# Latent attention's queries: rotary columns of four heads in one tile

## The chip, the core and the metric

The kernel runs on one core of a Trainium2 chip. The metric is the time of one execution on the device in microseconds, as the median of several runs. The core's engines are TensorE (PE in the profile; its weight loads are PEld), VectorE (DVE), ScalarE (ACT), GpSimd (POOL) and SyncE (SP). SP, ACT and POOL also issue transfers (DMA), each in its own queue and in order.

## What is computed

The reference is a two-layer encoder over 512 tokens with 1024 features. In each layer a feed-forward block is followed by three attention branches that are gated and merged, by a second feed-forward block and by a gated input embedding. The change lies in the first branch, latent attention with 16 heads:

```
q = (rms_norm(c_q, q_norm) @ w_uq).reshape(b, s, 16, 64 + 32)
q_nope, q_rope = q[..., :64], apply_rope(q[..., 64:], cos, sin)
k_rope = apply_rope(k_rope, cos, sin)                     # one for all heads
logits = (q_nope . k_nope + q_rope . k_rope) * 96 ** -0.5
```

`c_q` has 384 columns. `apply_rope` takes the 32 rotary columns as two halves x1, x2 of 16 and gives `[x1 cos - x2 sin, x2 cos + x1 sin]`.

## The kernel before

Tokens lie along the free dimension: a tile is 128 features by 512 tokens. Every matrix is split into a rounded part (`h`) and a remainder (`l`), and a product is three matmuls (`mm3`): high times high, low times high, high times low. A queries' tile of 128 features from the three tiles of `cq` takes nine matmuls of 128x512.

`mix` runs the attention branches of a layer. It walks over 16 heads of latent attention, then 8 and 16 heads of the other two. For each head it writes logits (`m0A4s` is layer 0, head 4, the logits of one block of queries), reduces, exponentials, transposes (`m0A4t`) and the product with the values (`m0A4o`). Between them it pumps projections out of a queue, the `Filler`: each has a due head, a name, its count of matmuls ("units") and a generator. `pace` derives from units and due heads how many matmuls go beside each head. The projections of latent attention are `mla_pair(j)` (queries `m0qa` and keys `m0kap` of heads 2j and 2j+1), `mla_v(g)` (values of four heads: four tiles `m0va` of six matmuls of 128x256) and `gate` (`m0ga`, 24 matmuls). Pair 0 and the first values are made before head 0; the other pairs become ready four steps ahead of their heads.

All projections write to PSUM banks of kind "a", of which there are three, taken in turn; logits, transposes and outputs share the five of kind "s". A tile waits until the last reader of its bank is done. ScalarE and VectorE never read a bank at the same time: where both read one, they take turns.

In `mla_pair` before, a head's tile holds its 64 own columns and, in the other half, its rotary columns twice: `[x1 x2 x2 x1]` for even heads, in front of the own columns for odd heads. One multiply by a table (`trig`) of cosines and sines, with the logits' scale in it, evacuates the tile; the key has its rotated columns twice in that half (`KA`, three sets), so the matmul adds the two products. Then the tile is split by ScalarE and VectorE. The keys' tile `m0kap` has two heads: per head ScalarE rounds a half (`m0ka00h`) and VectorE subtracts it (`m0ka00l`).

The weights of each projection come as a chunk of 128x1024 on SP's queue (`wraw`, line 88, four buffers), are rounded by ScalarE (`whi`, line 101) and subtracted by VectorE (`wlo`, line 107) or, during `mix`, negated by ScalarE (line 104) and completed by an adding transfer on POOL's queue (line 105).

The order of instructions on each engine is laid when the program is built, from the order in which the code issues them and from when the planner expects their inputs. On the chip every engine keeps that order.

Of the kernel before, what the change touches and what calls it, by code (L numbers as in the profile page):

```python
# [12 lines left out]
F32 = mybir.dt.float32  # L13
F32R = mybir.dt.float32r
AF = mybir.ActivationFunctionType
ALU = mybir.AluOpType
# [4 lines left out]
P = 128  # L21
D = 1024
KT = D // P
T = 512
# [4 lines left out]
NH = 16  # L29
NHD = 8  # L30
QL = 384
KVL = 256
SCALE_A = 96 ** -0.5
# [149 lines left out]
def encoder_kernel(ctx: ExitStack, tc: tile.TileContext, ins, out):  # L183
    nc = tc.nc
# [22 lines left out]
    def S(name, dt=F32):  # L207
        return sb.tile([P, 512], dt, tag="slot", name=name, bufs=SLOTS)
# [4 lines left out]
    turn = [0]  # L213

    def PS(name, kind=None):


        if kind is None:
            kind = CYCLE[turn[0] % len(CYCLE)]
            turn[0] += 1  # L220
        return psp.tile([P, 512], F32, tag="ps" + kind, name=name, bufs=BANKS[kind])
# [4 lines left out]
    def mm3(ps, lh, ll, rh, rl, start, stop):  # L226
        mm(ps, lh, rh, start, False)
        mm(ps, ll, rh, False, False)
        mm(ps, lh, rl, False, stop)

    def split(src, name, tile=None):

        tile = tile or S
        hi, lo = tile(name + "h", F32R), tile(name + "l", F32R)
        nc.scalar.copy(hi, src)
        nc.vector.tensor_sub(lo, src, hi.bitcast(F32))
        return hi, lo
# [12 lines left out]
    t = S("one")  # L250
# [11 lines left out]
    for l in range(L):  # L262
        for i, at in enumerate((S_F1, S_F2)):
            s = slice(l * 8 + 4 * i, l * 8 + 4 * i + 4)
# [147 lines left out]
    def proj(ps, w, z, i0=0, n=KT, cols=P):  # L412

        wh, wl = w
        for k in range(n):
            c = slice(i0 + k * cols, i0 + k * cols + cols)
            mm3(ps, wh[:, c], wl[:, c], z[k][0], z[k][1], k == 0, k == n - 1)
            if side:
                side.popleft()()
            yield 3  # L420
# [301 lines left out]
    def mix(l, prep, p2):  # L722
        name = f"m{l}"
# [3 lines left out]
        def kept(nm, dt=F32):  # L727
            return stage.tile([P, 512], dt, tag="kept", name=f"{name}{nm}", bufs=17)
# [16 lines left out]
        for d in range(KT):  # L745
            if d % 4 == 0:
                w = W.get(("ple_proj", l, d // 4))
            ps = PS(f"{name}pp{d // 4}{d % 4}")
# [12 lines left out]
        trig = [kept(f"trig{i}") for i in range(3)]  # L761
# [45 lines left out]
        cq, ckv, got = end_q(), [], {}  # L807
# [13 lines left out]
                ckv.extend(end_kv())  # L821

        merged = [None] * KT

        def mla_v(g):
            wh, wl = W.get(("mla_v", l, g))
            vs = [S(f"{name}va{g}_{tb}", F32R) for tb in range(TB)]
            for tb in range(TB):
                ps = PS(f"{name}va{g}_{tb}", "a")[:, 0:256]
                ts = slice(tb * P, (tb + 1) * P)  # L830
                for k in range(2):
                    w = slice(k * 256, (k + 1) * 256)
                    mm(ps, ckv[k][0][:, ts], wh[:, w], k == 0, False)
                    mm(ps, ckv[k][1][:, ts], wh[:, w], False, False)
                    mm(ps, ckv[k][0][:, ts], wl[:, w], False, k == 1)

                v = vs[tb].rearrange("p (g x c) -> p g x c", x=4, c=64)
                src = ps.rearrange("p (g e c) -> p g e c", e=2, c=64)
                nc.scalar.copy(v[:, :, 0::3, :], src)
                nc.vector.tensor_sub(v[:, :, 1:3, :], src, v[:, :, 0::3, :].bitcast(F32))  # L840
                yield 3
            got["va", g] = vs

        def mla_pair(j):
            wh, wl = W.get(("mla_pair", l, j))
            for e in range(2):
                ps = PS(f"{name}qa{j}{e}", "a")
                yield from proj(ps, (wh, wl), cq, i0=e * 384, n=3)
                t = S(f"{name}qa{j}{e}")
                nc.vector.tensor_mul(t, ps, trig[e])  # L850
                got["qa", 2 * j + e] = split(t, f"{name}qa{j}{e}")
            ps = PS(f"{name}kap{j}", "a")
            yield from proj(ps, (wh, wl), ckv, i0=768, n=2)
            for e in range(2):
                r = slice(0, 64) if e == 0 else slice(64, 128)
                kh, kl = KA[j % KSETS][e]
                nc.scalar.copy(kh[r], ps[r])
                nc.vector.tensor_sub(kl[r], ps[r], kh[r].bitcast(F32))

        halves = (slice(0, 64), slice(64, 128))  # L860

        def q_pair(key, at, j):

# [305 lines left out]


        A0, C0, B0, END = 0, NH, NH + NHD, 2 * NH + NHD
        work = [(A0 + 2 * j - 1, ("pair", j), 24, mla_pair(j)) for j in range(8)]
        work += [(A0 + 4 * g, ("va", g), 12, mla_v(g)) for g in range(4)]
        work += [(A0 + 2 * j + 1, ("ga", j), 24, gate("ga", C_GA, j)) for j in range(2, 8)]
        for j in range(8):
# [150 lines left out]
    for l in range(L):  # L1326
# [9 lines left out]
        ffn(l, "ffn1", prep, pm, hooks)  # L1336
        close_stage()
        sums, outs = mix(l, pm, p2)
        open_stage(True)
        pf = Combos(f"f2_{l}", l, S_F2)  # L1340
# [43 lines left out]
KSETS = 3  # L1384
# [13 lines left out]
def _chunk(ins, key):  # L1398

    kind, c = key[0], None  # L1400
    if kind == "cols":
        _, w, l, i = key
        c = ins[w][l][:, i * P:(i + 1) * P].reshape(KT, P, P)
    elif kind == "in":
        _, l, at = key
        c = ins["w_in"][l][:, at:at + P].reshape(KT, P, P)
    elif kind == "down":
        _, w, l, g, i = key
        rows = ins[w + "_w_down"][l][GROUPS[g].start * P:GROUPS[g].stop * P]
        n = rows.shape[0] // P  # L1410
        c = rows[:, i * (1024 // n):(i + 1) * (1024 // n)].reshape(n, P, 1024 // n)
    elif kind == "out":
        _, l, half, kk = key
        c = ins["w_out"][l][kk * 256:(kk + 1) * 256, half * 512:(half + 1) * 512].reshape(2, P, 512)
    elif kind == "rope":
        w = ins["w_in"][key[1]]
        c = np.concatenate([w[:, C_KR:C_KR + 32], w[:, C_KR + 16:C_KR + 32], w[:, C_KR:C_KR + 16]], axis=1).reshape(KT, P, 64)
    elif kind in ("vb", "vc"):
        l, kk = key[1], key[-1]
        at = C_VB if kind == "vb" else C_VC + key[2] * 256  # L1420
        c = ins["w_in"][l][kk * 512:(kk + 1) * 512, at:at + 256].reshape(4, P, 256)
    elif kind == "mla_v":
        _, l, g = key
        w = ins["mla_w_ukv"][l].reshape(KVL, NH, P)[:, 4 * g:4 * g + 4, 64:]
        c = w.reshape(2, P, 256)
    elif kind == "mla_pair":
        _, l, j = key
        parts = []
        for e in range(2):
            w = ins["mla_w_uq"][l][:, (2 * j + e) * 96:(2 * j + e + 1) * 96]  # L1430
            own, rope = w[:, :64], [w[:, 64:], w[:, 80:], w[:, 64:80]]
            w = np.concatenate([own] + rope if e == 0 else rope + [own], axis=1)
            parts.append(w.reshape(3, P, P))
        w = ins["mla_w_ukv"][l].reshape(KVL, NH, P)[:, 2 * j:2 * j + 2, :64].reshape(KVL, P)
        parts.append(w.reshape(2, P, P))
        c = np.concatenate(parts, axis=0)
    elif kind == "ple_proj":
        _, l, i = key
        c = ins["ple_w_proj"][l][:, i * 512:(i + 1) * 512].reshape(2, P, 4, P).transpose(2, 0, 1, 3).reshape(8, P, P)
    return c.transpose(1, 0, 2).reshape(P, -1)  # L1440


def _trig():
    inv = np.float32(10000.0) ** (-np.arange(0, 32, 2, dtype=np.float32) / np.float32(32))
    ang = np.arange(T, dtype=np.float32)[:, None] * inv.astype(np.float32)[None, :]
    cos, sin = np.cos(ang).T, np.sin(ang).T
    turn = np.concatenate([cos, cos, -sin, sin], axis=0)
    s = np.float32(-SCALE_A)
    own = np.full((64, T), s, np.float32)
    res = np.zeros((3, P, T), np.float32)  # L1450
    res[0] = np.concatenate([own, s * turn])
    res[1] = np.concatenate([s * turn, own])
    res[2, :64] = turn
    return res

# [70 lines left out]
```

## Time and profile before

| | |
|---|---|
| median of 3 runs | 2982.31 us (2982.14 to 2983.64) |
| profiled execution | 2985.1 us, span 2983.3 us, granted clock 0.997 |
| PE busy | 2920.9 us, 98% of the span |
| DVE, ACT, POOL busy | 70%, 60%, 29% |
| layer 0's latent attention | from about 430 us to about 700 us |
| layer 1's latent attention | from about 1905 us to about 2175 us |

The span is that of one profiled execution from its first to its last instruction. A row of the timeline has a start and a duration in microseconds, the engine, the line and the operation, then "output<-inputs" and the shape. In a group's row, "x16 | 10.9, 679 | 0.0" means 16 instructions, 10.9 us of busy time, 679 ns for one, and no idle time before them; a name after "<-" is what ended that idle time. A matmul's duration overlaps the next one's, so its pace is read from start to start. A row of waits gives the sum in microseconds, the number of times and the longest.

### The profile page before, as it was taken

The page shows a single profiled execution, that of the slowest core. Times are in us where ns is not written, and L with a number is a line of the kernel's source. Part 1 is how long each engine was busy: PE and PEld are TensorE (multiplying, and loading weights), DVE is VectorE, ACT ScalarE, POOL GpSimd, SP SyncE. Part 2 cuts the span into 40 slices and gives each one's busy share as a digit, 9 for nine tenths or more (in the row PEclk, how much of TensorE's full clock was granted, in tenths as well). Part 3 has the DMA queues.
Part 4 walks back from the last instruction along what each step waited for, and adds up shares of the span by engine and source line. Part 5 has one row for each costly group of instructions (what it writes and reads, how often), then busy time and mean ns, then how long its engine had stood idle before and what let it go on. Part 6 is the DMA issues. An engine that isn't in the chain of part 4 may idle for free. (4 is left out here: it accounts for less than half of the span.)

```text
span 2983.3 us, 45438 instructions
## 1 busy us (share of the span) xinstructions
PE 2920.9 (98%) x16812; PEld 2544.6 (85%) x16812; DVE 2079.9 (70%) x3515; ACT 1780.0 (60%) x3281; POOL 866.5 (29%) x1000
## 2 busy tenths in 40 slices
PE   8999999999999999999999999999999999999998
PEld 7989878888887888999889998788888888889996
DVE  7677776645787768767687776866467866676776
ACT  5444457767888855445454444677578888544443
POOL 1343103322333332322222331123223333322313
PEclk9999999999999999999999999999999999999999
DMA  6685335455555556553355645354555465655532
GB/s 209 160 253 157 120 123 134 100 134 138 142 128 122 139 147 196 158 142 106 120 161 150 178 106 171 95 121 111 134 135 149 103 149 132 185 161 147 154 96 85
DMA packets 133934, 421.45 MB, mean 141 GB/s; under 512 B 16174, under 2 KB 18542, under 8 KB 133712
## 3 DMA queue, kind: packets, MB, share of 16 engines
q0 software_dynamic: 53712, 156.01, 26.0%
q1 hardware_dynamic: 78272, 260.64, 25.7%
q8 instruction: 132, 2.16, 0.3%
q10 hardware_dynamic: 1728, 1.90, 0.2%
q14 instruction: 90, 0.74, 0.1%
HBM read 331.39 MB, written 18.94 MB: 117 GB/s over the span
## 5 line engine op out<-in xcount | busy, mean ns | idle before, releaser
L101 ACT CAST whi<-wraw 128x1024 fp32r<-128x1024 f32 x312 | 327.0, 1051 | 239.3 <-issue 55.0
L105 POOL DMA_DIRECT2D wlo<-wraw x146 | 126.8, 868 | 561.4 <-ACT wlo L104 470.8
L107 DVE TENSOR_TENSOR wlo<-wraw,whi 128x1024 fp32r<-128x1024 f32 x166 | 203.9, 1233 | 82.1 <-ACT whi L101 80.8
L104 ACT ACTIVATE wlo<-whi 128x1024 fp32r<-128x1024 f32 x146 | 154.9, 1061 | 2.1
L554 DVE SCALAR_TENSOR_TENSOR wo0h<-ffn11d,wo0h 128x512 f32<-128x512 f32 x48 | 33.0, 687 | 30.7 <-PE ffn11d L224 30.7
L554 DVE SCALAR_TENSOR_TENSOR wo0h<-ffn20d,wo0h 128x512 f32<-128x512 f32 x48 | 32.8, 687 | 29.5 <-PE ffn20d L224 29.5
L554 DVE SCALAR_TENSOR_TENSOR wo1h<-ffn21d,wo1h 128x512 f32<-128x512 f32 x48 | 32.8, 687 | 28.8 <-PE ffn21d L224 28.7
L554 DVE SCALAR_TENSOR_TENSOR x<-ffn10d,x 128x512 f32<-128x512 f32 x48 | 32.6, 686 | 27.4 <-PE ffn10d L224 27.3
L367 POOL TENSOR_TENSOR f_1sq<-f_1sq,f_1sq 128x512 f32<-128x512 f32 x14 | 21.4, 1528 | 49.3 <-ACT f_1sq L362 48.9
L917 ACT CAST m0kc<-m0kc 64x512 fp32r<-64x512 f32 x32 | 18.6, 582 | 15.0 <-PE m0kc L224 13.5
L917 ACT CAST m1kc<-m1kc 64x512 fp32r<-64x512 f32 x32 | 18.6, 582 | 14.9 <-PE m1kc L224 13.5
L870 DVE SCALAR_TENSOR_TENSOR m1qc<-m1qc,m1qc 64x512 fp32r<-64x512 f32 x16 | 11.0, 689 | 18.9 <-ACT m1qc L869 18.7
L870 DVE SCALAR_TENSOR_TENSOR m0qc<-m0qc,m0qc 64x512 fp32r<-64x512 f32 x16 | 11.0, 688 | 18.9 <-ACT m0qc L869 18.7
L1164 ACT ACT_TABLE_LOAD x16 | 20.5, 1283 | 0.3
L367 POOL TENSOR_TENSOR pg0sq<-pg0sq,pg0sq 128x512 f32<-128x512 f32 x7 | 10.6, 1513 | 23.9 <-ACT pg0sq L362 23.9
L367 POOL TENSOR_TENSOR pg1sq<-pg1sq,pg1sq 128x512 f32<-128x512 f32 x7 | 10.6, 1515 | 23.1 <-ACT pg1sq L362 23.1
L1348 POOL TENSOR_SCALAR out<-wo1h,small 128x512 f32<-128x512 f32 (+1 forms) x9 | 7.2, 799 | 32.5 <-DVE wo1h L1311 32.5
L938 DVE TENSOR_TENSOR m1vc<-m1vc,m1vc 128x256 fp32r<-128x256 f32 x16 | 6.4, 414 | 14.3 <-ACT m1vc L937 14.2
L938 DVE TENSOR_TENSOR m0vc<-m0vc,m0vc 128x256 fp32r<-128x256 f32 x16 | 6.4, 414 | 14.3 <-ACT m0vc L937 14.2
L869 ACT ACTIVATE m1qc<-m1qc 64x512 fp32r<-64x512 f32 x16 | 9.5, 592 | 10.4 <-PE m1qc L224 9.0
L869 ACT ACTIVATE m0qc<-m0qc 64x512 fp32r<-64x512 f32 x16 | 9.5, 592 | 10.4 <-PE m0qc L224 9.0
L224 PE MATMUL idle<-warm,ones 128*128 128x512 f32 x14 | 5.9, 603 | 8.5 <-DVE warm L254 8.5
(15134 smaller groups left out, 12591.9 us busy)
## 6 DMA issues: line engine op xcount, KB each, us to landing
wraw<-in_wall SPq DMA_DIRECT2D x312, 512.0 KB, 3.5
wlo<-wraw POOLq DMA_DIRECT2D x146, 512.0 KB, 4.6
copies_s<-bias_s POOLq DMA_DIRECT2D x16, 256.0 KB, 9.6
copies_d<-bias_d POOLq DMA_DIRECT2D x8, 512.0 KB, 10.7
h_dram<-x POOLq DMA_DIRECT2D x8, 256.0 KB, 2.7
pp_dram<-m0ppt POOLq DMA_DIRECT2D x8, 256.0 KB, 3.7
wo0h<-h_dram POOLq DMA_DIRECT2D x8, 256.0 KB, 7.1
ple0p<-pp_dram POOLq DMA_DIRECT2D x8, 256.0 KB, 4.4
```

What stands on the lines that cost most here:

```text
L101: pin(self.nc.scalar.copy(hi, raw))
L104: self.nc.scalar.activation(lo, hi.bitcast(F32), AF.Copy, scale=-1.0)
L105: self.nc.gpsimd.dma_start(lo.bitcast(F32), raw, accum_op=ALU.add)
L107: self.nc.vector.tensor_tensor(lo, raw, hi.bitcast(F32), op=ALU.subtract)
L367: self.engine.tensor_tensor(self.acc, self.acc, sq, op=ALU.add)
L554: nc.vector.scalar_tensor_tensor(h[d], ps, 0.5, h[d], op0=ALU.mult, op1=ALU.add)
L869: nc.scalar.activation(qs[e][own], ps[own], AF.Copy, scale=-0.125)
L870: nc.vector.scalar_tensor_tensor(qs[e][other], ps[own], -0.125, qs[e][own].bitcast(F32), op0=ALU.mult, op1=ALU.subtract)
L917: nc.scalar.copy(ks[e][r], ps[own])
L938: nc.vector.tensor_sub(t[:, 256:512], ps, t[:, 0:256].bitcast(F32))
L1164: nc.scalar.activation(r, ss, AF.Sqrt, bias=eps, scale=1.0 / P)
L1348: nc.gpsimd.tensor_scalar(gained[d][:, c], h[d][:, c], small[:, L * S_N + d:L * S_N + d + 1], 1.0, op0=ALU.mult, op1=ALU.mult)
```

## The change

A query head's rotary columns are no longer stored twice. The x1 and the x2 of four heads (4 x 2 x 16 = 128 columns) form one tile `m0qr0`, which only even pairs make, for heads 2j to 2j+3. VectorE turns it: one multiply by cosines, two of 64 partitions that read the other half of the tile, times sines, and an addition in SBUF. ScalarE and VectorE split the result. For each of the four heads four transfers of 16x512 in SBUF carry its rounded part and its remainder to the other half of the head's tile `m0qh0`, where the key has its rotated columns twice: the rounded part meets one copy, the remainder the other. The own columns of two heads form a second tile (`m0qa0`); per head ScalarE writes the rounded own half into `m0qh0`, VectorE the remainder into a tile of `QL`, whose other half six memsets on POOL set to zero once in a layer. So two pairs take three queries' tiles instead of four, twelve instead of sixteen in a layer. The weights are arranged for it on the host.

```
+        QL = [[S(f"{name}ql{s}{e}", F32R) for e in range(2)] for s in range(KSETS)]
+        for s in range(KSETS):
+            for e in range(2):
+                nc.gpsimd.memset(QL[s][e][halves[1 - e]].bitcast(F32), 0.0)
...
         def mla_pair(j):
             wh, wl = W.get(("mla_pair", l, j))
+            at = 0
+            if j % 2 == 0:
+                ps = PS(f"{name}qr{j}", "a")
+                yield from proj(ps, (wh, wl), cq, n=3)
+                at = 384
+                y, z = S(f"{name}qr{j}y"), S(f"{name}qr{j}z")
+                nc.vector.tensor_mul(y, ps, trig[0])
+                for e in range(2):
+                    nc.vector.tensor_mul(z[halves[e]], ps[halves[1 - e]], trig[1][halves[1 - e]])
+                nc.vector.tensor_add(y, y, z)
+                parts = split(y, f"{name}qr{j}")
+                for i in range(4):
+                    q = got["qh", 2 * j + i] = S(f"{name}qh{2 * j + i}", F32R)
+                    for x, part in enumerate(parts):
+                        for b in range(2):
+                            to = halves[1 - i % 2].start + 32 * x + 16 * b
+                            nc.sync.dma_start(q[to:to + 16].bitcast(F32), part[64 * b + 16 * i:64 * b + 16 * i + 16].bitcast(F32))
+            ps = PS(f"{name}qa{j}", "a")
+            yield from proj(ps, (wh, wl), cq, i0=at, n=3)
             for e in range(2):
-                ps = PS(f"{name}qa{j}{e}", "a")
-                yield from proj(ps, (wh, wl), cq, i0=e * 384, n=3)
-                t = S(f"{name}qa{j}{e}")
-                nc.vector.tensor_mul(t, ps, trig[e])
-                got["qa", 2 * j + e] = split(t, f"{name}qa{j}{e}")
+                own = halves[e]
+                qh, ql = got.pop(("qh", 2 * j + e)), QL[j % KSETS][e]
+                nc.scalar.activation(qh[own], ps[own], AF.Copy, scale=-SCALE_A)
+                nc.vector.scalar_tensor_tensor(ql[own], ps[own], -SCALE_A, qh[own].bitcast(F32), op0=ALU.mult, op1=ALU.subtract)
+                got["qa", 2 * j + e] = qh, ql
             ps = PS(f"{name}kap{j}", "a")
-            yield from proj(ps, (wh, wl), ckv, i0=768, n=2)
+            yield from proj(ps, (wh, wl), ckv, i0=at + 384, n=2)
...
-        work = [(A0 + 2 * j - 1, ("pair", j), 24, mla_pair(j)) for j in range(8)]
+        work = [(A0 + 2 * j - 1, ("pair", j), (24, 15)[j % 2], mla_pair(j)) for j in range(8)]
```

How the order moves is shown at two places of layer 0; layer 1 has the same.

VectorE at the start of the stage, before, from the last split of the keys' inputs (`m0ckv1l`) on. The first number behind a name tells buffers apart.

```order
L236 TENSOR_TENSOR m0ckv1l<-m0ckv_4217,m0ckv1h 128x512
L850 TENSOR_TENSOR m0qa_4344<-m0qa_4334,m0trig_3984 128x512
L236 TENSOR_TENSOR m0qa00l<-m0qa_4344,m0qa00h 128x512
L850 TENSOR_TENSOR m0qa_4360<-m0qa_4350,m0trig_3985 128x512
L858 TENSOR_TENSOR m0ka00l<-m0kap_4366,m0ka00h 64x512
L107 TENSOR_TENSOR wlo_4378<-wraw_4257,whi_4377 128x1024
L236 TENSOR_TENSOR m0qa01l<-m0qa_4360,m0qa01h 128x512
L858 TENSOR_TENSOR m0ka01l<-m0kap_4366,m0ka01h 64x512
L840 TENSOR_TENSOR m0va_0_4383<-m0va_0_4387,m0va_0_4383 128x2x128
```

The same place on VectorE after the change (lines are those of the changed file).

```order
L236 TENSOR_TENSOR m0ckv1l<-m0ckv_4217,m0ckv1h 128x512
L859 TENSOR_TENSOR m0qr0y<-m0qr_4346,m0trig_3984 128x512
L861 TENSOR_TENSOR m0qr0z<-m0qr_4346,m0trig_3985 64x512 x2
L885 TENSOR_TENSOR m0ka00l<-m0kap_4400,m0ka00h 64x512
L862 TENSOR_TENSOR m0qr0y<-m0qr0y,m0qr0z 128x512
L107 TENSOR_TENSOR wlo_4412<-wraw_4257,whi_4411 128x1024
L236 TENSOR_TENSOR m0qr0l<-m0qr0y,m0qr0h 128x512
L877 SCALAR_TENSOR_TENSOR m0ql_4328<-m0qa_4386,m0qh_4366 64x512
L885 TENSOR_TENSOR m0ka01l<-m0kap_4400,m0ka01h 64x512
L877 SCALAR_TENSOR_TENSOR m0ql_4329<-m0qa_4386,m0qh_4371 64x512
L1036 TENSOR_REDUCE m0A0m<-m0A0s_4459 128x1
```

The last reader of the second queries' tile was the multiply at the fourth row; now it is the second subtraction of the own columns (`m0ql_4329`), the last row but one, and the reduces of head 0 follow ahead of the values' subtractions. On PE the first four projections' tiles are in the same sequence (turned queries, own queries, `m0kap`, first values); behind them stood two blocks of head 0's logits and then the second values, and now stand the second and third values and then the logits.

ScalarE beside pair 2, before: `m0kap_4620` is the keys' tile of that pair, `m0A0pth` the copies of head 0's transposes.

```order
L235 CAST m0qa20h<-m0qa_4562 128x512
L958 CAST m0A0pth_4580<-m0A0t_4575 128x512
L958 CAST m0A0pth_4589<-m0A0t_4584 128x512
L958 CAST m0A0pth_4598<-m0A0t_4593 128x512
L958 CAST m0A0pth_4607<-m0A0t_4602 128x512
L857 CAST m0ka20h<-m0kap_4620 64x512
L101 CAST whi_4631<-wraw_4381 128x1024
L235 CAST m0qa21h<-m0qa_4614 128x512
L104 ACTIVATE wlo_4632<-whi_4631 128x1024
L857 CAST m0ka21h<-m0kap_4620 64x512
```

The same place on ScalarE after the change.

```order
L884 CAST m0ka20h<-m0kap_4622 64x512
L235 CAST m0qr2h<-m0qr2y 128x512
L101 CAST whi_4669<-wraw_4415 128x1024
L876 ACTIVATE m0qh_4571<-m0qa_4591 64x512
L884 CAST m0ka21h<-m0kap_4622 64x512
L104 ACTIVATE wlo_4670<-whi_4669 128x1024
L876 ACTIVATE m0qh_4576<-m0qa_4591 64x512
L1038 ACTIVATE m0A1p_4603,m0A1s<-m0A1s_4598,m0A1m 128x512
L1038 ACTIVATE m0A1p_4613,m0A1s<-m0A1s_4608,m0A1m 128x512
L983 CAST m0A0pth_4631<-m0A0t_4626 128x512
```

The copies of head 0's transposes stood ahead of the keys' halves and now stand behind them, behind both own halves of the queries and behind two exponentials of head 1. On PE the second group of values comes directly behind `m0kap_4622`, and its second tile takes the bank of `m0qa_4591`.

More of the change, by code (lines that the diff above doesn't have):

```diff
@@ L823, in mix @@
         merged = [None] * KT
+        halves = (slice(0, 64), slice(64, 128))
+        QL = [[S(f"{name}ql{s}{e}", F32R) for e in range(2)] for s in range(KSETS)]
+        for s in range(KSETS):
+            for e in range(2):
+                nc.gpsimd.memset(QL[s][e][halves[1 - e]].bitcast(F32), 0.0)
         def mla_v(g):
@@ L858, in mla_pair @@
                 nc.vector.tensor_sub(kl[r], ps[r], kh[r].bitcast(F32))
-        halves = (slice(0, 64), slice(64, 128))
         def q_pair(key, at, j):
@@ L1427, in _chunk @@
         _, l, j = key
[L1428 to L1433, printed above, removed]
+        w = ins["mla_w_uq"][l].reshape(QL, NH, 96)
+        parts = [w[:, 2 * j:2 * j + 2, :64].reshape(3, P, P)]
+        if j % 2 == 0:
+            w = w[:, 2 * j:2 * j + 4, 64:].reshape(QL, 4, 2, 16).transpose(0, 2, 1, 3)
+            parts.insert(0, w.reshape(3, P, P))
         w = ins["mla_w_ukv"][l].reshape(KVL, NH, P)[:, 2 * j:2 * j + 2, :64].reshape(KVL, P)
@@ L1448, in _trig @@
     s = np.float32(-SCALE_A)
-    own = np.full((64, T), s, np.float32)
     res = np.zeros((3, P, T), np.float32)
-    res[0] = np.concatenate([own, s * turn])
-    res[1] = np.concatenate([s * turn, own])
+    res[0] = np.tile(s * cos, (8, 1))
+    res[1] = np.concatenate([np.tile(s * sin, (4, 1)), np.tile(-s * sin, (4, 1))])
     res[2, :64] = turn
```

## The prediction

> **What bounds the kernel now.** I read the page's busy shares first, then stretches of the stage that the change touches, then the chain of waits, and last the rows of the timeline around the edited code.
>
> ```profile
> span 2983.3 us, 45438 instructions
> PE 2920.9 (98%) x16812; PEld 2544.6 (85%) x16812; DVE 2079.9 (70%) x3515; ACT 1780.0 (60%) x3281; POOL 866.5 (29%) x1000
> ...
> 430.00:470.00 40.00, 38.19 (x193) 31.05 (x192) 31.28 (x52) 31.89 (x59) 9.92 (x12) 1.00 0.45 118
> 470.00:510.00 40.00, 38.79 (x205) 32.13 (x204) 25.55 (x45) 29.51 (x57) 12.38 (x16) 1.00 0.52 120
> 510.00:700.00 190.00, 188.40 (x1015) 160.87 (x1014) 102.86 (x179) 128.26 (x238) 52.22 (x66) 1.00 0.51 120
> ...
> 2669.81 21.79 PE ffn21d L224 x96
> ```
>
> The three stretches hold latent attention's sixteen heads in layer 0 (columns: PE, PEld, DVE, ACT, POOL, then granted clock, DMA share, GB/s). PE idles 1.8, 1.2 and 1.6 us in them, so a matmul less is worth its pace here, and a PE wait more costs its whole length. The chain's row gives the pace: 96 matmuls of 128x512 in 21.79 us, 0.227 us each. In the first 40 us DVE and ACT are busy 78% and 80%: there PE has little cover.
>
> **What is removed.** Four odd pairs per layer lose one tile of nine matmuls: 4 x 9 x 2 layers = 72, times 0.227 = 16.3 us, if PE does nothing worse. The filler's units fall with it (24 to 15), so its pace shares the saving over the heads instead of emptying one.
>
> **What is added to DVE and ACT.** Two pairs had four turns and four splits; they get one turn (three multiplies and an addition), one split, and four halves that ScalarE rounds and VectorE subtracts. The nearest rows for such halves are those of q_pair:
>
> ```profile
> L869 ACT ACTIVATE m0qc<-m0qc 64x512 fp32r<-64x512 f32 x16 | 9.5, 592 | 10.4 <-PE m0qc L224 9.0 <-DVE m0qc L870 1.2
> L870 DVE SCALAR_TENSOR_TENSOR m0qc<-m0qc,m0qc 64x512 fp32r<-64x512 f32 x16 | 11.0, 688 | 18.9 <-ACT m0qc L869 18.7
> L850 DVE TENSOR_TENSOR m0qa<-m0qa,m0trig 128x512 f32<-128x512 f32 x16 | 10.9, 679 | 0.0
> 460.36 0.67 DVE L850 TENSOR_TENSOR m0qa<-m0qa,m0trig 128x512 f32<-128x512 f32 x1
> 460.96 0.67 DVE L858 TENSOR_TENSOR m0ka20l<-m0kap,m0ka20h 64x512 fp32r<-64x512 f32 x1
> ```
>
> DVE starts one such instruction every 0.60 us. By count it is 8 x 0.60 before against 9 x 0.60 now for two pairs: as throughput nothing. What matters is who holds a PSUM bank. Before, a queries' tile was free after one multiply. Now the turned tile is free after three, and the other after ACT, DVE, ACT, DVE in turn: the rows above show ACT's second half waiting for DVE (1.2 us <-DVE L870) and DVE for ACT. Kind "a" has three banks, and the values' tiles come next in them:
>
> ```profile
> L224 PE MATMUL m0va<-whi,m0ckv0h 128*128 128x256 f32 x16 | 4.9, 306 | 2.2 <-DVE m0ka11l L858 1.2 <-DVE m0qa L850 0.9
> L224 PE MATMUL m1va<-whi,m1ckv0h 128*128 128x256 f32 x16 | 4.9, 305 | 2.2 <-DVE m1ka11l L858 1.2 <-DVE m1qa L850 0.9
> 436.83 0.39 PE L224 MATMUL m0kap<-m0ckv1l,whi 128*128 128x512 f32 x1
> 437.06 0.28 PE L224 MATMUL m0va<-whi,m0ckv0h 128*128 128x256 f32 x1
> 437.17 0.28 PE L224 MATMUL m0va<-whi,m0ckv0l 128*128 128x256 f32 x1
> ```
>
> PE's only waits of this kind were 1.2 and 0.9 us a layer, the latter for a turned query tile: that fixes which bank the next values' tile takes. A values' matmul takes 0.12 us.
>
> **Start of the stage, worked out.** Rows of DVE and ACT there:
>
> ```profile
> 435.87 0.68 DVE L850 TENSOR_TENSOR m0qa<-m0qa,m0trig 128x512 f32<-128x512 f32 x1
> 439.05 1.21 DVE L107 TENSOR_TENSOR wlo<-wraw,whi 128x1024 fp32r<-128x1024 f32 x1
> 440.18 0.68 DVE L236 TENSOR_TENSOR m0qa01l<-m0qa,m0qa01h 128x512 fp32r<-128x512 f32 x1
> 437.26 0.58 ACT L857 CAST m0ka00h<-m0kap 64x512 fp32r<-64x512 f32 x1
> 437.74 1.04 ACT L101 CAST whi<-wraw 128x1024 fp32r<-128x1024 f32 x1
> 438.69 0.62 ACT L235 CAST m0qa01h<-m0qa 128x512 fp32r<-128x512 f32 x1
> ```
>
> Everything ahead of 435.87 on DVE is as before, so the turn's first multiply starts there, the next two at 436.47 and 437.07, done 437.74. The first values' tile takes the turned tile's bank: 437.78 in place of 437.06, **0.72 us**. Then DVE does the keys' half (its cast ends at 437.84) at 437.88, the addition at 438.48, a weight split at 439.08 (1.13 to the next start), the turned split at 440.21 and the first own half at 440.82, done 441.51. ACT can then round the second half (0.59), DVE subtract it (0.69): done 442.87. The second values' tile waits for that bank. PE is there at 438.50 and goes on at 442.91: **4.41 us**. Two values' tiles later, at 444.34, PE reaches head 0's logits. The fourth values' tile wants the first one's bank, whose subtraction stands behind four reduces that follow the logits 0.68 us apart: it ends at about 448.28, PE is there at 447.74: **0.57 us**.
>
> **Pair 2, beside the second group of values.** ACT's order is now key half, turned tile, weight, own half, key half, weight, own half, all after the last matmul of kap. Prices:
>
> ```profile
> 458.65 0.60 ACT L857 CAST m0ka20h<-m0kap 64x512 fp32r<-64x512 f32 x1
> 459.13 1.07 ACT L101 CAST whi<-wraw 128x1024 fp32r<-128x1024 f32 x1
> 461.07 0.62 ACT L235 CAST m0qa21h<-m0qa 128x512 fp32r<-128x512 f32 x1 [0.87 <-DVE m0qa L850]
> 461.60 1.05 ACT L104 ACTIVATE wlo<-whi 128x1024 fp32r<-128x1024 f32 x1
> 462.67 0.58 ACT L857 CAST m0ka21h<-m0kap 64x512 fp32r<-64x512 f32 x1
> ```
>
> Start to start: 0.48 + 0.53 + 0.95 + 0.48 + 0.48 + 1.0, then 0.59 for the last half, 0.69 on DVE and some 0.1 of handing over: 5.3 us. Kap's last result comes 0.16 us after PE may go on, and PE has one values' tile (0.72) to fill it: 4.75 us of waiting where 0.9 stood: **3.8 us**. Head 0's copies for its output now stand behind these on ACT too; the last values of head 0 then follow at the pace of PE.
>
> **Pairs 4 and 6.** The same chain is shorter (key half, weight, own half, DVE: 0.16 + 0.48 + 0.95 + 0.59 + 0.69 + 0.1 = 3.0 us) and PE has a values' tile, three or six logits matmuls and four transposes (about 1.8 or 2.5 us). That leaves 1.2 us, where 1.2 us stood already, and 0.5 us; the fourth values' tile of each group may wait again behind reciprocals. I take **2.0 us** for both, between 0 and 4.0. Odd pairs are followed by a gate of 24 matmuls (5.4 us): nothing.
>
> **Transfers.** 16 for each turned tile, on SP's queue, 64 a layer.
>
> ```profile
> L88 SPq DMA_DIRECT2D wraw<-in_wall x10: 327/328/328, 433.7 to 498.0; - x10
> out<-out SPq DMA_DIRECT2D x8, 128.0 KB, 2.0
> wlo<-wraw POOLq DMA_DIRECT2D x146, 512.0 KB, 4.6
> SPq L88 <- DMA wlo<-wraw: 1223.2, 146, 23.4
> ```
>
> Nothing in the trace is 32 KB from SBUF to SBUF: 2.0 us is the nearest in size, 4.6 us (which also adds) the nearest in kind. Head 0 needs four. The last is issued at about 441.6 and lands at 443.6 by the first, before PE's 444.34: **nothing**, because the bank's wait covers it; if that wait were gone, the transfers would hold PE to 443.6 instead. By the second they add 1.9 us a layer. Later heads have a whole head's time. Weight loads behind them slip by 16 x 0.33 = 5.3 us; SP's loads already wait 1223 us for slots and keep four slots ahead: nothing. The six memsets run while POOL is idle.
>
> **Sum.** Per layer 0.72 + 4.41 + 0.57 + 3.8 + 2.0 = 11.5 us, with 9.5 and 13.5 by the bounds of pairs 4 and 6. Layer 1 has the same order: 23.0. Net 23.0 - 16.3 = +6.7 us. The profiled execution took 2985.1 us (span 2983.3), 2.8 above the median of 2982.31; from the median: 2989.0 us.
>
> **Rivals.**
> 1. *The long waits don't come* (faster): PE's waits of 4.41 and 3.8 us vanish, 16.4 us in both layers: 2972.6. For it speaks only that the order was laid by a planner that had other choices; against it, the bank rotation seen above. It decides below 5.2 us of new waiting a layer (16.3 - 6, halved).
> 2. *Half of them*: one of the two long waits is mostly covered: about 2981, no change.
> 3. *Transfers late*: 4.6 us each: +3.8, 2992.8.
> 4. *The clock falls in the gaps*:
>
> ```profile
> 8.50 5.91 PE L224 MATMUL idle<-warm,ones 128*128 128x512 f32 x14 [8.50 <-DVE warm L254]
> 14.24 0.40 PE L224 MATMUL ffn10g<-f_0z0h,whi 128*128 128x512 f32 x1
> ...
> PE finss L377 <- DVE finsq L373: 2.7, 2, 2.4
> ```
>
> After 8.5 us of idling 14 matmuls take 5.91 us, 0.42 each against 0.227: 2.7 us lost. PE's next longest wait, at the program's end, is 2.4 us; the new ones would be 4.4 and 4.75 us. If each of the four costs that, 10.8 us more: 2999.8; with two, 2994.4. The Trainium skill speaks against the change here: "TensorE: Matmul & The Clock Gate" (Part 1, the HAM clock gate) says that the array falls to half rate after an idle window of about 3.4 us, which runs free of the program. By that rule some of the four gaps would be hit, not all.
>
> **How the numbers follow.** My forecast, 2989.0 (own range 2985 to 2993), has 0.45; rival 1 0.12; rival 2 0.18; rival 3 0.10; rival 4 0.15. Within 0.2% (6 us, about what a measurement of this kernel tells from no change) means 2976.3 to 2988.3. Rivals 3 and 4 and some 0.27 of the forecast lie above: slower 0.52; rival 2 and the rest of the forecast: same 0.36; faster 0.12. The range, 2976 to 3000, leaves out rival 1 and the end of rival 4.
>
> **What would show it.** PE's waits on m0va (DVE, m0ql) near 4.4 us at the stage's start and near 4.7 us at the second group of values, and the same on m1va; PE busy about 16 us less, PE idle in 430 to 510 up from 3.0 to some 12 us; logits waiting for no DMA; the granted clock in those stretches at 1.00 or below it. I am wrong if the stretch's idle time grows by less than 5 us a layer, or if PE waits for transfers or weights instead.

## The result, and the profile after

The changed kernel takes 3014.06 us (median of 4 runs, 3011.71 to 3014.95) against 2982.74 us before on the same chip: a ratio of 1.0097, 95% interval 1.0084 to 1.0109. It is 31 us slower; the forecast was 7 us slower. The experiments ran on three chips, where the kernel before took 2985 to 2987 us, so they are told as ratios to it: the changed kernel's 1.0097 is what they are held against. A few executions there, of the kernel before too, took 4800 to 8900 us; the ratios leave them out.

First the page's head, then the same three stretches of layer 0's latent attention (columns: PE, PEld, DVE, ACT, POOL, granted clock, DMA share, GB/s).

```profile
span 3011.9 us, 45656 instructions
PE 2920.7 (97%) x16740; PEld 2541.2 (84%) x16740; DVE 2087.0 (69%) x3523; ACT 1786.3 (59%) x3289; POOL 865.7 (29%) x1012
...
430.00:470.00 40.00, 30.84 (x137) 24.04 (x136) 29.70 (x48) 25.86 (x46) 5.96 (x9) 0.91 0.40 107
470.00:510.00 40.00, 39.89 (x196) 33.22 (x196) 24.41 (x43) 28.57 (x57) 11.48 (x15) 0.97 0.63 144
510.00:700.00 190.00, 178.55 (x942) 150.45 (x941) 101.41 (x177) 128.24 (x238) 49.67 (x65) 0.98 0.49 118
```

The span grew by 28.6 us. PE has 72 matmuls less, but its busy time is what it was (2920.7 against 2920.9 us; the forecast had 16 us less): the 16 us that they took are lost to a slower pace (granted clock 0.91, 0.97 and 0.98 here, 1.00, 1.00 and 1.00 before). And PE idles 91.2 us in place of 62.4. In the three stretches it idles 9.2, 0.1 and 11.5 us, before 1.8, 1.2 and 1.6.

PE's waits from 425 to 760 us (sum, times, longest):

```profile
PE m0ga L224 <- DVE m0va L846: 5.4, 1, 5.4
PE m0va L224 <- DVE m0ka01l L885: 4.2, 2, 3.5
PE m0va L224 <- DVE m0ka21l L885: 3.4, 1, 3.4
PE m0va L224 <- DVE m0ql L877: 2.0, 2, 1.3
PE m0A3o L224 <- ACT m0A3pth L983: 1.5, 1, 1.5
...
PE m0va L224 <- DVE m0qr0z L861: 0.8, 1, 0.8
PE m0va L224 <- DVE m0va L846: 0.7, 1, 0.7
```

Three of them were forecast in place, and nearly in size: the first values' tile waits for the turn's multiplies (0.8 us, forecast 0.72), the second for a half (3.5, forecast 4.41, but for a half of another tile, as the account below says), the fourth for its predecessor (0.65 of 0.7, forecast 0.57). The second values wait 3.4 us (forecast 4.75). The largest, 5.4 us at a gate, and the 1.5 us of head 3's output were not forecast at all. Layer 1 has the same waits, with 4.8 us at its gate.

The timeline says what the gate's wait is. Followed back over VectorE and ScalarE it ends at an exponential. This exponential, and likewise a copy of head 3, waited for a transfer:

```profile
574.91 0.69 ACT L1038 ACTIVATE m0A8p<-m0A8s,m0A8m 128x512 f32<-128x512 f32 x1 [5.44 <-DMA m0qh<-m0qr6h]
522.41 1.56 ACT L983 CAST m0A3pth<-m0A3t 128x512 fp32r<-128x512 f32 x3 [4.70 <-DMA m0qh<-m0qr4h]
575.99 0.76 DVE L846 TENSOR_TENSOR m0va<-m0va,m0va 128x256 fp32r<-128x256 f32 x2
576.47 0.79 PE L224 MATMUL m0ga<-m0m0u0h,whi 128*128 128x512 f32 x1 [5.45 <-DVE m0va L846]
```

Neither instruction uses a query. They write a new tile, and its place in SBUF is one of the 62 slots of the common pool: the one that the turned tile's rounded part `m0qr6h` (for head 3, `m0qr4h`) had, which its eight transfers were still reading. The rest follows down the row: ScalarE stands, so the values' halves behind it stand, so the bank that the gate needs is not free. The transfers themselves, by line (min/median/max ns of the issue, first and last start):

```profile
L870 SPq DMA_DIRECT2D m0qh<-m0qr6h x8: 512/557/1566, 563.0 to 572.2; - x8
L870 SPq DMA_DIRECT2D m0qh<-m0qr6l x8: 526/587/703, 564.2 to 574.1; - x8
DMA to landing us min/median/max: 1.9/2.0/5.4
```

A landing takes the 2.0 us that was assumed (median). But SP spends 0.51 to 0.59 us on most issues and up to 1.57 us on a few, not 0.33 as on a weight load, and there are sixteen in one queue, rounded parts and remainders by turns: from 563.0 to 574.7 us.

The lower clock sits behind the long waits (timeline of PE, and its stretches with the granted clock after the busy time):

```profile
443.83 0.55 PE L224 MATMUL m0va<-whi,m0ckv0h 128*128 128x256 f32 x1 [3.49 <-DVE m0ka01l L885]
...
447.80 0.63 PE L224 MATMUL m0A0s<-m0ka00h,m0qh 128*128 128x512 f32 x1
448.23 0.63 PE L224 MATMUL m0A0s<-m0ka00h,m0ql 128*128 128x512 f32 x1
...
449.43 0.40 PE L224 MATMUL m0A0s<-m0ka00l,m0qh 128*128 128x512 f32 x1
...
444.00:449.00 5.00, 5.00 (x19) 0.52 0.22 51
577.00:583.00 6.00, 6.00 (x18) 0.59 0.49 114
```

From start to start a 128x512 matmul takes 0.43 us after the wait, and its duration is 0.63 us; from 449 us on it is 0.40 us, as before, at 0.23 us from start to start. The 18 matmuls behind the start's wait lost 2.35 us (12 took 2.69 in place of 1.42, six 2.45 in place of 1.37), the 13 behind the gate's 2.65 (5.61 in place of 2.96), those behind the second values' wait some 1.4 (12 took 2.94 in place of 1.43, with a gap of 0.08 among them). That is 6.4 us in layer 0, and 5.9 in layer 1 by the same reckoning: 12 of the 16 us. This is the forecast's fourth rival, and it came on top of the forecast, not in its place. The Trainium skill, "TensorE: Matmul & The Clock Gate" (Part 1, the HAM clock gate), gives half rate after an idle window of about 3.4 us; the half pace agrees, and the waits of 3.4 to 5.45 us were all followed by it.

### The profile page after: what moved, and what is told of

Read it like the earlier page. It is cut to its first block, busy times and chain, and to the rows that moved or that the text cites. A ratio compares the mean times of both kernels' runs of the same rounds, so it can differ in the third digit from the quotient of the medians.

```text
span 3011.9 us, 45656 instructions
## 1 busy us (share of the span) xinstructions
PE 2920.7 (97%) x16740; PEld 2541.2 (84%) x16740; DVE 2087.0 (69%) x3523; ACT 1786.3 (59%) x3289; POOL 865.7 (29%) x1012
## 5 line engine op out<-in xcount | busy, mean ns | idle before, releaser
L224 PE MATMUL m0va<-whi,m0ckv0h 128*128 128x256 f32 x16 | 6.1, 383 | 11.1 <-DVE m0ka01l L885 4.2
L894 ACT ACTIVATE m0qc<-m0qc 64x512 fp32r<-64x512 f32 x16 | 9.5, 594 | 11.1 <-PE m0qc L224 7.5
L894 ACT ACTIVATE m1qc<-m1qc 64x512 fp32r<-64x512 f32 x16 | 9.5, 593 | 11.1 <-PE m1qc L224 7.5
```

The source lines that it names most:

```text
L224: nc.tensor.matmul(ps, lhsT, rhs, start=start, stop=stop, skip_group_check=True)
L894: nc.scalar.activation(qs[e][own], ps[own], AF.Copy, scale=-0.125)
```

## The experiments

The theory after the result: three costs of about equal weight. *Slots*: transfers hold an SBUF slot for as long as SP issues them. *Banks*: halves in turn hold PSUM banks at the start and at the second values. *Clock*: matmuls behind a long wait run at half pace. The rival to each is that its wait only hides another.

**1. Idle matmuls in the gaps (clock).**

```
 ps = PS(f"{name}va{g}_{tb}", "a")[:, 0:256]
+if (g, tb) == (0, 1):
+    dummy = PS(..., "s")
+    for i in range(14): mm(dummy, ckv[0][0][:, 0:P], ckv[0][0], i == 0, i == 13)
...
+if g == 2: (22 of them after the group's last tile)
```

> The changed kernel with idle matmuls of 128x512 into a bank of kind s that nobody reads: 14 a layer ahead of the second values' tile at the stage's start, 22 ahead of the gate at which PE waited 5.4 us. All other instructions keep their order. Clock theory: the two gaps stay, but TensorE works in them, so the matmuls behind them run at full pace. Behind the first gap 12 values' matmuls took 2.69 us (1.42 at 0.119 us each) and 6 of the logits 2.45 us (1.37), behind the gate's gap 13 took 5.61 us (2.96): 5.0 us a layer, 10 us in both, so about 3004 us against 3014. Rival (the slow pace comes from something else, or the idle matmuls only delay): 3014 us or more, with the slow matmuls as before.

Ratio 1.0083 (1.0069 to 1.0096): some 4 us less than the changed kernel, not 10, and the two intervals overlap. At the start it did what was expected:

```profile
443.34 0.36 PE L224 MATMUL m0va<-whi,m0ckv0h 128*128 128x256 f32 x1 [1.47 <-DVE m0ka01l L894]
...
444.00:449.00 5.00, 4.86 (x24) 1.00 0.21 48
515.78 5.18 PE L224 MATMUL m0dm<-m0ckv0h 128*128 128x512 f32 x22
```

With 1.47 us of idling left in place of 3.49, 24 matmuls start in the 5 us behind it at clock 1.00, where 19 did at 0.52. But the other 22 were put at the wrong group of values, one gate too early (515.8 us), where they cost 5 us of PE's time. The total says little; the stretch shows that idling, not the work, sets the pace.

**2. Own slots (slots).** The turned tile's two parts get a slot each of their own, the common pool has 60; the planner moved some instructions around heads 3, 7, 8 and 10.

```
-parts = split(y, f"{name}qr{j}")
+parts = split(y, f"{name}qr{j}", lambda nm, dt: sb.tile([P, 512], dt, tag="qr" + nm[-1], name=nm, bufs=1))
-SLOTS = 62
+SLOTS = 60
```

> The changed kernel with two SBUF slots of their own for the turned tile's rounded part and remainder (the common pool has 60 in place of 62). Slot theory: ScalarE's exponential of head 8 waited 5.4 us, and a copy of head 3's transposes 4.7 us, because they write into the slot that the 16 transfers of a turned tile were still reading; PE's waits of 5.45 us at the gate and 1.5 us at head 3's output go, and the slow matmuls behind the first (2.6 us) with them: 9.6 us a layer, 19 us in all, about 2995 us. Rival (the banks alone are to blame, ScalarE is late anyway): PE waits at the gate for something else, and less than 3 us are won.

Ratio 1.0043 (1.0030 to 1.0057): 16 us less, forecast 19. The exponential now waits 0.56 us, for a transpose, and PE waits 0.6 us at the gate:

```profile
573.31 0.69 ACT L1038 ACTIVATE m0A8p<-m0A8s,m0A8m 128x512 f32<-128x512 f32 x1 [0.56 <-PE m0A7t L980]
PE m0ga L224 <- DVE m0va L846: 0.6, 1, 0.6
PE m0va L224 <- DVE m0ql L877: 5.0, 2, 4.8
474.12 0.41 PE L224 MATMUL m0va<-whi,m0ckv0h 128*128 128x256 f32 x1 [2.67 <-DVE m0ka21l L885]
474.10:477.00 2.90, 2.88 (x14) 0.53 0.86 246
```

With the slot its wait went, and what hung on it: that cost is shown, up to the instructions that the planner moved. The start is worse than before (4.8 us, now for the own queries' half), and the second values still wait 2.67 us. The last two rows show the half pace after an idle time of 2.67 us.

**3. One read out of the bank (banks).**

```
-nc.scalar.activation(qh[own], ps[own], AF.Copy, scale=-SCALE_A)
-nc.vector.scalar_tensor_tensor(ql[own], ps[own], -SCALE_A, qh[own].bitcast(F32), ...)
+t = S(...); nc.scalar.activation(t, ps, AF.Copy, scale=-SCALE_A)     # once a pair
+nc.scalar.copy(qh[own], t[own])
+nc.vector.tensor_sub(ql[own], t[own], qh[own].bitcast(F32))
...the same for the keys' tile, with t of its own
```

> The changed kernel, but ScalarE copies the own queries' tile and the keys' tile out of PSUM whole (two copies of 128x512, 0.6 us each, a pair), and the halves are rounded and subtracted from that copy in SBUF. Bank theory: the bank is free after one read, not after four in turn. The 3.49 us wait at the start falls to some 1.6 us (the copies stand behind a weight and the turned tile on ScalarE), the 3.37 us at the second values to some 0.6, and the slow matmuls behind both (2.35 and 1.3 us) go: 8 us a layer, 16 in all, about 2998 us. Rival (ScalarE, 78% busy there, is the bound, not the bank): the waits stay or grow, 3014 us or more.

Ratio 1.0138 (1.0122 to 1.0153): 12 us worse than the changed kernel, the rival's number. The rows tell where the time goes:

```profile
443.06 0.39 PE L224 MATMUL m0va<-whi,m0ckv0h 128*128 128x256 f32 x1 [2.46 <-ACT m0qt L876]
446.73 0.76 PE L224 MATMUL m0A0s<-m0ka00h,m0qh 128*128 128x512 f32 x1 [1.56 <-DMA m0qh<-m0qr0l]
469.22 1.11 PE L985 MATMUL m0A0t<-ident,m0A0p 128*128 128x128 f32 x4 [3.23 <-ACT m0A1p L1043]
...
578.60 0.59 ACT L885 COPY m0kt<-m0kap 128x512 f32<-128x512 f32 x1 [5.02 <-DMA m0qh<-m0qr6h]
579.24 0.58 PE L224 MATMUL m0va<-whi,m0ckv0h 128*128 128x256 f32 x1 [6.29 <-ACT m0kt L885]
```

The longest wait, 6.29 us, is the slot's cost again: the keys' copy is a new tile of the pool, and it waited 5.02 us for the transfers of `m0qr6h`. At the start the bank did come free earlier (2.46 us in place of 3.49), but head 0's logits then waited 1.56 us for their transfers. At the second values the wait of 3.37 us moved to head 0's transposes (3.23 us), behind an exponential on ScalarE; transposes of later heads waited for exponentials too (1.8, 1.1, 0.7 and 0.6 us, against 0.2 in the changed kernel). There ScalarE is the bound, as the rival says, though one of these exponentials had itself waited 2.4 us for a transfer. So one read freed the first bank earlier, and PE met the next wait; the 12 us were not taken apart further. (ScalarE's share of 430 to 470 us is 65% in the changed kernel, 25.86 of 40.00 us, not the expectation's 78%.)

**4. The gain alone.** The kernel before, with 72 queries' matmuls left out.

```
-yield from proj(ps, (wh, wl), cq, i0=e * 384, n=3)
+yield from proj(ps, (wh, wl), cq, i0=e * 384, n=3 if j % 2 == 0 else 2 - e)
-("pair", j), 24, mla_pair(j))
+("pair", j), (24, 15)[j % 2], mla_pair(j))
```

> The kernel before, with 72 queries' matmuls left out: in odd pairs the two heads' tiles take six and three matmuls in place of nine each, and the pair's units are 15. Everything that evacuates them stays. It prices the gain alone. Forecast: 72 x 0.227 = 16.3 us, about 2966.4 us against 2982.7. Rival (PE loses its cover where VectorE and ScalarE are the bound): half of it, 2974 us, with new waits on PE in the stage.

Ratio 0.9915 (0.9901 to 0.9928): 25 us, more than the count gives. The same edit again, to see where the rest is won:

> The kernel before with 72 queries' matmuls left out once more, as its first profile showed an execution of 7884 us. 25 us were won there (ratio 0.9915) where the count gives 16.3. If the 9 us beyond come from PE's waits in the stage: idle time of PE over the whole span lower by some 9 us than the 62 us before, at places where a queries' tile or its bank was waited for. Rival (the order of other work changed with the pairs' units): the same stretch around the pairs idles as before, and the time is won in later stages.

Ratio 0.9916 (0.9902 to 0.9929). Over the span PE's busy time falls by 15.8 us (to 2905.1), near the 16.3 of the count, and its idle time by 6.6 (from 62.4 to 55.8). Where that is, layer 0 shows: from the first matmul of `m0cq` to the first of `m0A15o`, and from there to the first of `m0B15o`, first before, then this run:

```profile
380.60:728.20 347.60, 342.04 (x1741) 283.07 (x1741) 214.12 (x355) 233.21 (x422) 83.73 (x108) 1.00 0.49 123
728.20:1069.80 341.60, 335.54 (x1806) 283.21 (x1805) 248.89 (x546) 278.40 (x570) 117.37 (x166) 1.00 0.54 132
...
384.40:722.80 338.40, 335.01 (x1711) 277.49 (x1711) 213.68 (x355) 233.31 (x423) 82.62 (x108) 1.00 0.51 127
722.80:1060.70 337.90, 332.86 (x1801) 281.04 (x1800) 248.39 (x546) 278.24 (x571) 117.22 (x166) 1.00 0.55 132
```

The first stretch is 9.2 us shorter, with 30 matmuls less (7.0 us of busy time) and 2.2 us less idling; the second 3.7 us, with 5 matmuls less, since the order of the filler's work moved across the border (2.7 us), and 1.0 us less idling. So the expectation and its rival each hold in part: two thirds of the idling that went, went in latent attention, one third in the stage behind it. The changed kernel has the gain of the later stage too: 337.8 us for the second stretch in layer 0, 339.2 against 342.8 in layer 1. So what is to be explained is not 31 + 16 us but some 54 (ratio 1.0097 against 0.9915), nearly all of it in latent attention (table below).

**5. Banks of the other kind (banks).** On top of own slots, even pairs' own queries and keys go to kind "s".

```
-ps = PS(f"{name}qa{j}", "a")
+ps = PS(f"{name}qa{j}", "s" if j % 2 == 0 else "a")
-ps = PS(f"{name}kap{j}", "a")
+ps = PS(f"{name}kap{j}", "s" if j % 2 == 0 else "a")
```

> The kernel with own slots for the turned tile's parts, and even pairs' own queries and keys write to PSUM banks of kind s, so that the values' tiles find the banks of kind a free. Bank theory: PE's waits for the values' tiles at the start (4.8 us in the run with own slots, 0.65 for the fourth tile) and at the second values (2.7 us) go, and the slow matmuls behind them (2.35 and 1.2 us); the logits of head 0 may then wait some 1.5 us for the transfers: about 9 to 10 us a layer, 18 to 20 us in all against the kernel with own slots (2998.6), so about 2980 us, level with the kernel before. Rival (kind s is as short: logits and transposes wait for the halves in its place): PE waits for logits or transposes by as much, 2995 us or more.

Ratio 1.0042 (1.0030 to 1.0055), the same as with own slots alone: the rival's size, by two mechanisms.

```profile
PE m0A0s L224 <- DMA m0qh<-m0qr0l: 5.1, 1, 5.1
PE m0A0t L980 <- DVE m0ql L877: 2.4, 1, 2.4
441.28 0.58 PE L224 MATMUL m0va<-whi,m0ckv0h 128*128 128x256 f32 x1 [2.07 <-DVE m0qr0z L861]
441.66 0.41 PE L224 MATMUL m0va<-whi,m0ckv0l 128*128 128x256 f32 x1
```

The long waits of the values' tiles are gone, so it was a bank that PE waited for. But at the start PE now waits 2.07 us for the turn's multiplies (and goes on at half pace), then 5.1 us at head 0's first logits, for its transfers; at the second values it waits 2.4 us for a bank of kind "s". The chain behind (turn, split, transfers) is the bound; the bank only was the first place where PE met it.

**6. Two queues (slots).**

```
-nc.sync.dma_start(q[to:to + 16]..., part[...])
+(nc.sync, nc.gpsimd)[x].dma_start(q[to:to + 16]..., part[...])     # x = 1: remainders
```

> The changed kernel with the remainders' eight transfers of a turned tile issued on POOL's queue, the rounded parts' eight stay on SP's; slots as in the changed kernel. Slot theory: SP took 0.56 to 0.6 us for each of 16, so the rounded part's slot was held some 12 us; with eight on each queue it is free after some 5 us, ScalarE's exponential waits 0 to 1 us in place of 5.4, and the gate's wait goes with it: 14 to 19 us less than the changed kernel, about 2997 us. Rival (the landing, not the issue, holds the slot; or POOL issues slower than SP, with its adding transfers in the same queue): less than 5 us less, 3009 us or more.

Ratio 1.0008 (0.9999 to 1.0017): 27 us less than the changed kernel (forecast 14 to 19), level with the kernel before, and 10 us better than own slots.

```profile
L870 SPq DMA_DIRECT2D m0qh<-m0qr6h x8: 513/554/590, 559.4 to 563.8; - x8
L870 POOL DMA_DIRECT2D m0qh<-m0qr6l x8: 484/484/533, 560.7 to 565.7; - x8
PE m0va L224 <- DVE m0ka01l L885: 4.2, 2, 3.5
PE m0va L224 <- DVE m0ql L877: 3.5, 3, 1.5
```

Eight rounded parts are issued in 5 us, and no instruction of ScalarE waits for a transfer any more. The start is as before (3.5 us); at the second values two waits, of 1.49 and 0.63 us, stand for the one of 3.4, and the matmuls behind keep their pace. There the planner also laid the turn of pair 2 earlier on VectorE, so what of the 10 us is order and what is slots was not separated. The Trainium skill, "DMA: Bandwidth & Descriptors" (Rules for kernel authors), says that spreading transfers over queues only saves the sequencer's issue time; the trace agrees (a landing's median is 2.1 us, before 2.0), and that time was not small here: eight issues in 5 us on each queue, in place of sixteen in 11.7 us.

**7. Work to cover the start.** Gate 2, due later, is made between pair 0 and the first values.

```
-fill.need(("pair", 0), ("va", 0))
+fill.need(("pair", 0))
+item = next(x for x in fill.queue if x[1] == ("ga", 2))
+while item in fill.queue: fill._step(item)
+fill.need(("va", 0))
```

> The changed kernel with one edit at the stage's start: the 24 matmuls of gate 2, which are due later in the stage anyway, are made between pair 0 and the first values (5.4 us of PE's work). It covers the chain that PE waited for there: turn, split, halves and keys on VectorE and ScalarE. Start theory: the waits at the start (0.8 + 3.5 + 0.65 us) and the slow matmuls behind them (2.35 us) go, less 0.8 for the gate's own bank: 6.5 us a layer, 13 us, about 3001 us against 3014. Rival (the work is taken from where it covered something else, or the next wait, for the transfers, comes in its place): less than 5 us.

Ratio 1.0062 (1.0050 to 1.0075): 10 us less, forecast 13.

```profile
440.27 0.50 PE L224 MATMUL m0ga<-m0m0u0h,whi 128*128 128x512 f32 x1 [0.78 <-DVE m0qr0z L861]
...
447.29 0.40 PE L224 MATMUL m0A0s<-m0ka00h,m0qh 128*128 128x512 f32 x1
```

Behind the gate PE goes through values and logits without a wait and at full pace; the transfers have landed. The control is the same edit on the kernel before:

> The control: the kernel before with gate 2 brought forward in the same way. PE has no wait at the stage's start there (0.9 us in all), so by the start theory nothing is won: 2984 us within 4. If the order itself is better, it is faster than before by more than 5 us, and what the gate wins for the changed kernel is not all the start's.

Ratio 0.9992 (0.9983 to 1.0001): nothing that can be told from no change, so most of the 10 us at least are the start's.

**8. Both together.** Two queues and the gate.

> Two queues for the transfers and gate 2 brought forward, both together. If slots and start are two separate costs, they add: 25 us (two queues, measured) and 13 us (gate, forecast) off the changed kernel's 3014, so about 2976 us, and faster than the kernel before by 0.3%. If they overlap: 2985 us or more.

Ratio 0.9982 (0.9973 to 0.9991): 34 us less than the changed kernel and 5 us (0.18%) faster than the kernel before. The two gains nearly add (27 and 10 alone). The waits left on PE from 425 to 760 us are short, and the clock is 0.98 or more. Where two of them, 1.82 and 0.73 us, fall within 4 us (at the second values), the half pace still comes (last two rows):

```profile
430.00:470.00 40.00, 35.73 (x174) 28.86 (x173) 31.36 (x50) 29.27 (x53) 13.73 (x24) 0.98 0.48 131
510.00:700.00 190.00, 187.76 (x1012) 160.16 (x1013) 104.86 (x183) 132.69 (x246) 56.77 (x78) 1.00 0.54 128
PE m0va L224 <- DVE m0ql L877: 3.9, 3, 1.8
468.32 0.55 PE L224 MATMUL m0va<-whi,m0ckv0h 128*128 128x256 f32 x1 [0.73 <-DVE m0ka21l L885]
468.68 0.41 PE L224 MATMUL m0va<-whi,m0ckv0l 128*128 128x256 f32 x1
```

With own slots besides:

> As the run with two queues and the gate, and with own slots for the turned tile's two parts (pool of 60). If two queues already free the slots in time, own slots give nothing more: 2976 us within 3. If some writers still wait for slots, a few us less.

Ratio 0.9995 (0.9986 to 1.0004): nothing more. Two queues already free the slots in time.

**9. Idle matmuls at the right gate (clock).** As in 1, with `g == 3`.

> As the first run with idle matmuls, but the 22 stand where PE waits 5.45 us for the slot (behind the values' tiles of the last group, ahead of the gate), not ahead of an earlier gate as they did there; 14 again at the stage's start. Every other instruction keeps the changed kernel's order, and both gaps keep their length, so all that is won is the pace behind them: 2.35 and 2.65 us a layer, 10 us, about 3004 us against 3014. Rival (the first run's 4 us are all there is): 3010 us or more.

Ratio 1.0088 (1.0074 to 1.0103): the rival's number, for a reason that no theory had. The idle matmuls needed a bank of kind "s", and that was held by the same exponential:

```profile
573.83 7.26 PE L224 MATMUL m0dm<-m0ckv0h 128*128 128x512 f32 x22 [4.51 <-ACT m0A8p L1047]
...
574.00:581.00 7.00, 7.00 (x23) 0.71 0.53 133
581.00:587.00 6.00, 6.00 (x28) 1.00 0.34 100
```

They came behind the gap and took the half pace on themselves (22 in 7.1 us, 5.0 at 0.227), and the gate after them ran at 1.00. So the slow pace goes with the gap and not with the gate's matmuls; what it costs in the total there was not measured by itself.

## Why the prediction was wrong

The stage from `m0cq` to `m0A15o` took, in layers 0 and 1 (differences of first starts, from the traces):

| | layer 0 | layer 1 |
|---|---|---|
| before | 347.6 us | 347.4 us |
| gain alone | 338.4 | 338.2 |
| changed | 365.5 | 362.7 |
| own slots | 355.6 | 356.1 |
| two queues | 352.4 | 352.1 |
| gate forward | 359.3 | 357.9 |
| two queues, gate forward | 346.8 | 348.9 |

Against the gain alone the change costs 27.1 and 24.5 us a layer; the forecast had 11.5. The step of the forecast that failed is "Transfers: nothing".

- **The gain** (16.3 us) was too small: 25 us, since PE also idled less, in latent attention and behind it (experiment 4). The matmuls' own price was right: 15.8 us of busy time.
- **The start** (0.72 + 4.41 + 0.57) was near in its waits: 0.79, 3.49, 0.65. For the second of them that is partly luck, as the rotation of the banks was misread: the tile took the keys' bank (released by `m0ka01l`), not the own queries'. In experiment 2, where it did wait for the own queries' half, the wait was 4.8 us. The forecast let the transfers hold PE to 443.6 us if the bank did not; experiments 3 and 5, where PE waits 1.56 and 5.1 us for them and starts head 0's logits at 446.7 and 448.0 us (446.5 in the changed kernel), show that this second bound lies as late as the first.
- **The second values** (4.75 us) were 3.37, again for the keys' half (`m0ka21l`), not for the own queries' bank that the section on the change names.
- **Pairs 4 and 6** (2.0 us above before) had waits of 1.3, 0.7 and 0.7 us at the values' tiles, within the bounds of 0 to 4.
- **"Transfers: nothing"** is the failed step. It asked when the queries land ("later heads have a whole head's time", which was right), and at 0.33 us an issue. It did not ask who wants the source's slot. The issue took some 0.57 us, the slot was held for some 12 us, and an exponential that has nothing to do with queries waited 5.4 us for it; PE waited 5.45 us at the gate behind that. With own slots the total fell by 16 us, with two queues by 27. The weight loads behind the transfers slipped by more than the forecast's 5.3 us, and PE waited for none of them longer (1.3 us at `m0vc`, before 1.2): there "nothing" was right.
- **The clock** was a rival with 0.15 and up to 10.8 us. It came in every long wait, and took some 6 us a layer by the rows above, 12 in both. A wait of 3 us and more should have had it in the sum, not beside it.
- **"Odd pairs are followed by a gate of 24 matmuls: nothing"** held: PE has one wait at a gate in layer 0, and that gate stands behind the last values, beside pair 6.

By the rows the forecast's waits (4.9 at the start, 3.4, 2.8 for pairs 4 and 6) make 11.1 us in layer 0, the gate and head 3's output 6.9 and the half pace 6.4: 24.4 us, or 23.6 without the wait of 0.8 us that the gain alone has there too, of 27.1 us. The rest was not traced to single rows.

## What to carry to other kernels

A transfer that reads SBUF keeps its source's slot until the last of its issues has landed: price a batch of small transfers by issues times issue time, and look for the next writer of that slot, which may be any instruction of the pool. A wait on PE is to be priced with the slow matmuls behind it. Where a new chain is the bound, freeing banks only moves the wait down the chain; work that is due later anyway, brought forward, covers it.

## What the runs showed of the hardware

Small transfers from SBUF to SBUF (16x512, 32 KB) mostly cost 0.51 to 0.59 us each on SP's queue, against 0.33 for a weight load of 512 KB, and 0.48 on POOL's. PE's half pace was seen right behind idle times of 2.07 us (experiment 5, granted clock 0.50) and 2.67 us (experiment 2, 0.53), and behind waits of 1.82 and 0.73 us close together (experiment 8); waits of 1.47 us (experiment 1) and 1.78 us (experiment 2, at 519.8 us) were not followed by it. The Trainium skill's rule ("TensorE: Matmul & The Clock Gate", Part 1, the HAM clock gate) speaks of an idle window of about 3.4 us; no single wait had to be as long as that here.
